# w_down's last four runs: low parts of raw blocks by DMA, and another order of the work at the ends of runs

## The chip, the cores and the metric

The kernel runs on one core of a Trainium2 chip. The metric is the device time of one execution in microseconds, here the median of several runs. A profiled execution has its own time and its own trace.

## The reference

One encoder layer on 512 tokens of width 2048, in float32: RMSNorm, one projection `w_in`, two groups of mixing heads (windowed attention at three dilations, gated linear attention in both directions), `w_out` and a residual; then RMSNorm, a SwiGLU feed-forward part and a residual; then a final RMSNorm. What matters here is the second half of the feed-forward part:

```python
h = rmsnorm(x, ffn_norm_w[l])
x = x + (jax.nn.silu(h @ w_gate[l]) * (h @ w_up[l])) @ w_down[l]
...
return rmsnorm(x, final_norm_w)
```

The hidden width is 5632, so `w_down` is 5632 by 2048 and the product to be formed is 512 x 5632 x 2048.

## The kernel before, in words

Every float32 operand of a matmul is written as a high part (a rounded copy, type float32r, made on ScalarE) and a low part (what is left, made on VectorE or by a DMA), and a product is three matmuls: high by high, high by low, low by high (lines 1591, 1592, 1593).

`w_down` is done in three stretches. Four ordinary jobs take the first four k-tiles of 128 rows, the class `Down` takes k-tiles 4 to 35 in pairs, and the last k-tiles are ordinary jobs and the tail again (`later_first`, `tail_first`). `Down` uses a scheme of Strassen's kind: a pair of k-tiles (2 x 128 rows), 512 columns of `w_down` and the 512 tokens are cut in halves each, and instead of eight block products seven are formed, of sums of blocks. Seven PSUM banks hold the seven products of one column block of 512. One **piece** is one pair of k-tiles in one column block: 7 products x 2 token halves x 3 matmuls = 42 matmuls of 128 x 256.

The pieces stand in **runs**; a run adds pieces of one column block into the seven banks. There are ten runs with 6, 6, 6, 11, 5, 5, 10, 5, 5 and 5 pieces, 64 in all (`self.runs`, `self.seq`). A column block has two runs or, in the case of blocks 1 and 2, three: the earlier ones end in `evac`, which copies each bank to SBUF and sends it to the DRAM tile `md` (added there by an accumulating DMA from the second time on); its last one, runs 6 to 9 (`summed`), begins with the sums so far, fetched from `md` (`fetch`, SyncE's queue) and copied into the banks (`preload`, ScalarE), and ends in `combine`: VectorE and ScalarE form the four output blocks from the seven banks, and `residuals` adds them to `x1`. `combine` and the `preload` of the next run alternate in the last piece of a run, since there are eight banks: a bank is refilled when `combine` has read it.

The weights of a piece go through these steps, each in buffers of the pool `s4` (20 buffers of 128 x 1024 floats):

- `load`: a raw block, 512 KB, by SyncE's queue; at most `self.most` raw blocks are alive.
- `sums(i)`: three additions on VectorE (lines 1130 to 1132) make four sums of the raw block's quarters.
- `split(i)`: high and low part of the raw block and of the sums. In the base class (lines 1142, 1147) both high parts are ScalarE copies and both low parts VectorE subtractions. For pieces for which `by_dma(i)` holds, `part(i)` has made the raw block's two parts earlier: ScalarE writes the negated rounded block (line 1481), an accumulating DMA of POOL's queue adds the raw block to it (line 1482), ScalarE writes the high part (line 1483); `split` then makes only the parts of the sums (lines 1493, 1494).
- `products(i)`: the 42 matmuls; then the piece's four part buffers go back to the pool. The raw block and the sums go back in `split`.

The pool hands out buffers in the order of the program (`Slots.get`): the first free one that was last used for the same kind, else the one free longest. An instruction that writes a buffer waits on the chip until the readers of the former content have ended, DMAs among them. Each engine and each queue works in the order in which `Down.run` issues.

`Down.run` goes over the pieces. For piece i it prepares the sums of i+2, the split of i+1 and the part of i+3, with one more of each where the pool has room, then advances `operands` (`make`; the activation's operands, which end in run 6), fetches the sums and `x1` for a run's end, issues `products(i)` and one step of `urgent` work (two `residuals`). In the last run it also begins the later jobs' weights through the stream `st`: `st.load` reads a raw block of two halves, `st.split` makes a half's parts (lines 201 and 202).

Of the kernel before, what the change touches and what calls it, by code (L numbers as in the profile page):

```python
# [114 lines left out]
def put(*slots):  # L115
    for s in slots:
        if s.home is not None:
            s.home.free.append(s.i)


def layer(nc, tc, x, attn_norm_w, w_in, rel_table, gw_f, gb_f, gw_b, gb_b, gla_norm_w, w_out,
# [4 lines left out]
    pe, act, dve, pool, sp = nc.tensor, nc.scalar, nc.vector, nc.gpsimd, nc.sync  # L126
    mm = pe.matmul

    with tc.manual_schedule(), \
# [7 lines left out]
        s4 = Slots(p4, N4, 1024, "b")  # L137
# [71 lines left out]
        st = Stream()  # L209
# [25 lines left out]
        def run_urgent():  # L235
            while urgent:
                try:
                    next(urgent[0])
                    break
                except StopIteration:  # L240
                    urgent.popleft()
# [20 lines left out]
        def job(kind, pieces, kts, acts, evac, rate=0.0, before=None, start=None, limit=None):  # L262

            j = Job()
            j.kind, j.kts, j.acts, j.evac, j.rate, j.before, j.start, j.limit = \
                kind, kts, acts, evac, rate, before, start, limit
            j.first = len(st.halves)
            st.add(pieces)
            j.n = len(st.halves) - j.first
            jobs.append(j)  # L270
            return j
# [1112 lines left out]
        def g_load(j):  # L1384
            if j < FF // 256 and j not in graw and 2 * j not in gT and j >= state["g"]:
                state["g"] = j + 1
                graw[j] = s4.get(F32, [P, 2, 512])
                sp.dma_start(out=graw[j].t.rearrange("p f t -> p (f t)"), in_=gd[j])
# [62 lines left out]
        class Down(Blocks):  # L1451
# [17 lines left out]
                return r >= 6  # L1469

            def by_dma(self, i):
                return i < self.n and self.seq[i][0] in (3, 6)

            def part(self, i):
                if not self.by_dma(i) or i in self.parts or i in self.sets:
# [92 lines left out]
            def products(self, i):  # L1568
                r, q = self.seq[i]
                c, part = self.runs[r]  # L1570
                (rh, rl), (sh, sl) = st_ = self.sets.pop(i)
                R = lambda n: (rh.t[:, 0, n], rl.t[:, 0, n])
                Z = lambda n: (sh.t[:, 0, n], sl.t[:, 0, n])
                first, last = q == part[0], q == part[-1]
                ahead = last and r + 1 < len(self.runs) and self.summed(r + 1)
                if first:
                    self.banks, self.pre = self.pre, []
                loaded = self.summed(r)
                if ahead:
                    self.preload(0)  # L1580
                x_ = self.x[q]
                prods = [(R(0), "B11"), (R(2), "B21"), (Z(2), "T2"), (Z(1), "T1"), (Z(0), "T3"), (Z(3), "B22"),
                         (R(1), "T4")]
                for n, ((wh, wl), x) in enumerate(prods):
                    if first and not loaded:
                        self.banks.append(ps.get())
                    xh, xl = x_[x]
                    for h in range(2):
                        o = self.banks[n].t[:, h * 256:(h + 1) * 256]
                        t = slice(h * P, (h + 1) * P)  # L1590
                        mm(o, xh[:, t], wh, start=first and not loaded and h == 0, stop=False, skip_group_check=True)  # L1591
                        mm(o, xh[:, t], wl, start=False, stop=False, skip_group_check=True)  # L1592
                        mm(o, xl[:, t], wh, start=False, stop=last, skip_group_check=True)  # L1593
                    if last:
                        if loaded:
                            self.combine(c, n, self.banks[n])
                        else:
                            self.evac(c, n, self.banks[n])
                        if ahead and n < 6:
                            self.preload(n + 1)  # L1600
                for hi, lo in st_:
                    put(hi, lo)
                if self.drop[q] == r:
                    put(*self.x.pop(q)["slots"])

            def evac(self, c, n, bank):

                y = s2.get()
                act.copy(y.t, bank.t)
                put(bank)  # L1610
                if (c, n) in self.seen:
                    pool.dma_start(out=md[7 * c + n], in_=y.t, accum_op=OP.add)
                else:
                    pool.dma_start(out=md[7 * c + n], in_=y.t)
                self.seen.add((c, n))
                put(y)
# [41 lines left out]
            def run(self):  # L1658
                for i, (r, q) in enumerate(self.seq):
                    c, part = self.runs[r]  # L1660
                    n = part.index(q)
                    self.load()
                    self.sums(i)
                    self.split(i)
                    self.sums(i + 1)
                    self.sums(i + 2)
                    self.split(i + 1)
                    self.part(i + 3)
                    if r not in (3, 6) and len(s4.free) > (6 if self.summed(r) else 4):
                        self.sums(i + 3)  # L1670
                        self.split(i + 2)
                    self.reserve = 11 if r in (4, 5) else 4
                    while q not in self.x:
                        self.reserve = 0
                        self.make(1)
                    self.make((r in (3, 6)) + i % 2)
                    if n == len(part) - 4 and r + 1 < len(self.runs) and self.summed(r + 1):
                        self.fetch(r + 1)
                    if self.summed(r) and n == len(part) - 2:
                        x1[c] = [s2.get() for _ in range(4)]  # L1680
                        for t in range(4):
                            pool.dma_start(out=x1[c][t].t, in_=xd[4 * c + t])
                    self.products(i)
                    run_urgent()
                    if r == len(self.runs) - 1:
                        if n == 0:
                            g_load(LAST // 2 - 2)
                        if n == 2:
                            g_split(LAST // 2 - 2)
                            g_load(LAST // 2 - 1)  # L1690
                            st.until, st.limit = None, 1
                            st.load()
                        if n > 2:
                            st.split(later_first + n - 2)
                st.limit, st.big = 3, tail_first

        def evac_later(c):
# [26 lines left out]
        later_first = len(st.halves)  # L1724
# [113 lines left out]
```

## Time and profile before

| | us |
|---|---|
| median of 3 runs | 2203.69 (2202.8 to 2204.0) |
| profiled execution | 2204.33 |
| its span, first to last instruction | 2202.6 |
| TensorE (PE) busy in the span | 2183.5 |
| VectorE (DVE) busy | 1552.0 |
| ScalarE (ACT) busy | 1201.6 |
| GpSimd (POOL) busy | 322.5 |
| `Down`, first to last matmul | 1774.9 to 2104.7 |

The granted TensorE clock was 0.998 over the span. In the rows of the table by stretches stand the stretch, its length, busy time and number of instructions (x) of PE, PEld (weight loads), DVE, ACT and POOL, then the granted clock, the DMA engines' mean busy share and GB/s. In timelines stand start, duration, engine, line, operation, output<-inputs, shapes, and in brackets the idle time before it and what ended it. In waits stand: who waited at which line <- for whom, total us, number of waits, the longest. Buffers are named by letters: `a` is the pool `s2`, `b` the pool `s4`, `pu` the PSUM banks. Matmuls are pipelined: a matmul shown with 0.28 us begins 0.12 us after the one before it.

### The profile page before, as it was taken

The page shows a single profiled execution, that of the slowest core. Times are in us where ns is not written, and L with a number is a line of the kernel's source. Part 1 is how long each engine was busy: PE and PEld are TensorE (multiplying, and loading weights), DVE is VectorE, ACT ScalarE, POOL GpSimd, SP SyncE. Part 2 cuts the span into 40 slices and gives each one's busy share as a digit, 9 for nine tenths or more (in the row PEclk, how much of TensorE's full clock was granted, in tenths as well). Part 3 has the DMA queues.
Part 4 walks back from the last instruction along what each step waited for, and adds up shares of the span by engine and source line. Part 5 has one row for each costly group of instructions (what it writes and reads, how often), then busy time and mean ns, then how long its engine had stood idle before and what let it go on. Part 6 is the DMA issues. An engine that isn't in the chain of part 4 may idle for free.

```text
span 2202.6 us, 33125 instructions
## 1 busy us (share of the span) xinstructions
PE 2183.5 (99%) x12374; PEld 1908.7 (87%) x12374; DVE 1552.0 (70%) x2699; ACT 1201.6 (55%) x2005; POOL 322.5 (15%) x356
## 2 busy tenths in 40 slices
PE   9999999999999999999999999999999999999998
PEld 7888888888888888888888888888888899999986
DVE  4366665755445446888888888888888896869975
ACT  5344444544445336666666666666666665666542
POOL 0000000000000011222222222222222112121100
PEclk9999999999999999999999999999999999999999
DMA  6525635242324434789889898898888976888642
GB/s 208 160 65 159 170 90 141 84 126 66 96 67 152 154 106 105 186 193 210 204 194 209 193 214 195 200 213 196 211 195 206 274 187 186 240 217 246 225 171 77
DMA packets 255457, 373.99 MB, mean 170 GB/s; under 512 B 17951, under 2 KB 179407, under 8 KB 255296
## 3 DMA queue, kind: packets, MB, share of 16 engines
q1 hardware_dynamic: 188768, 252.03, 36.4%
q0 software_dynamic: 65344, 118.80, 27.6%
q8 instruction: 97, 1.59, 0.3%
q10 hardware_dynamic: 1184, 1.06, 0.1%
q14 instruction: 64, 0.52, 0.1%
HBM read 246.58 MB, written 35.19 MB: 128 GB/s over the span
## 4 chain that ended last, share of the span: by engine, by line
PE 94%; DVE 3%; ACT 1%; issue 1%; DMA 1%; POOL 0%; SPq 0%; ACTq 0%; POOLq 0%; DVEq 0%
PE pd L1275 22%; PE pd L1281 11%; PE ps L303 5%; PE ps L295 5%; PE ps L305 5%; PE ps L304 5%; PE ps L296 5%; PE ps L297 5%; PE pu L1592 4%; PE pu L1591 4%; PE pu L1593 4%; PE pe L1275 4%; PE pe L1281 2%; PE ps L529 1%; PE pu L304 1%; PE pu L305 1%
## 5 line engine op out<-in xcount | busy, mean ns | idle before, releaser
L1275 PE MATMUL pd<-a,b 128*128 128x512 f32 x2112 | 528.4, 392 | 0.1
L1275 PEld LDWEIGHTS pd<-a,b 128*128 128x128 f32 x2112 | 379.0, 188 | 66.3 <-DVE a L1036 0.5
L1281 PEld LDWEIGHTS pd<-a,b 128*128 128x128 f32 x2112 | 288.5, 190 | 21.5
L1281 PE MATMUL pd<-a,b 128*128 128x256 f32 x2112 | 294.9, 282 | 0.0
L1182 POOL DMA_DIRECT2D b<-b x176 | 209.7, 1248 | 521.8 <-ACT b L1181 393.7
L202 DVE TENSOR_TENSOR a<-b,a 128x512 fp32r<-128x512 f32 x288 | 192.5, 686 | 131.1 <-ACT a L201 130.9
L1220 ACT CAST b<-b 128x1024 fp32r<-128x1024 f32 x176 | 185.4, 1053 | 166.6 <-DVE b L1206 138.4
L1592 PE MATMUL pu<-b,a 128*128 128x256 f32 x896 | 253.9, 283 | 2.4 <-DVE b L1147 1.9
L1591 PE MATMUL pu<-b,a 128*128 128x256 f32 x896 | 254.5, 284 | 1.8 <-ACT pu L1564 1.8
L1593 PE MATMUL pu<-b,a 128*128 128x256 f32 x896 | 253.5, 283 | 0.0
L1221 DVE TENSOR_TENSOR b<-b,b 128x1024 fp32r<-128x1024 f32 x176 | 214.8, 1221 | 50.7 <-ACT b L1220 26.4
L201 ACT CAST a<-b 128x512 fp32r<-128x512 f32 x288 | 169.4, 617 | 48.8 <-PE ps L305 22.3
L1591 PEld LDWEIGHTS pu<-b,a 128*128 128x128 f32 x896 | 171.9, 192 | 3.5 <-ACT pu L1564 3.5
L1592 PEld LDWEIGHTS pu<-b,a 128*128 128x128 f32 x896 | 171.9, 192 | 3.1 <-DVE b L1147 2.1
L1593 PEld LDWEIGHTS pu<-b,a 128*128 128x128 f32 x896 | 171.9, 192 | 0.0
L1303 DVE TENSOR_TENSOR a<-pd,a 128x512 f32<-128x512 f32 x132 | 91.4, 692 | 96.5 <-ACT a L1302 96.5
L1181 ACT ACTIVATE b<-b 128x768 fp32r<-128x768 f32 x176 | 149.1, 847 | 4.7 <-PE ps L305 2.9
L1183 ACT CAST b<-b 128x768 fp32r<-128x768 f32 x176 | 145.2, 825 | 0.6 <-PE ps L305 0.6
L1302 ACT COPY a<-pd 128x512 f32<-128x512 f32 x132 | 77.5, 587 | 103.2 <-PE pd L1281 103.2
L1203 DVE TENSOR_TENSOR b<-b 128x512 f32<-128x512 f32 x176 | 120.3, 684 | 0.0
L1142 ACT CAST b<-b 128x768 fp32r<-128x768 f32 x86 | 77.1, 942 | 77.6 <-issue 46.9
L593 ACT CAST b<-ps 128x512 fp32r<-128x512 f32 x64 | 37.6, 587 | 144.7 <-PE ps L529 142.8
(256 smaller groups left out, 4454.6 us busy)
## 6 DMA issues: line engine op xcount, KB each, us to landing
b<-b POOLq DMA_DIRECT2D x197, 384.0 KB, 5.4
b<-in_w_gate_dram SPq DMA_DIRECT2D x88, 512.0 KB, 3.9
b<-in_w_up_dram SPq DMA_DIRECT2D x88, 512.0 KB, 4.6
b<-in_w_down_dram SPq DMA_DIRECT2D x88, 512.0 KB, 5.6
b<-in_w_in_dram SPq DMA_DIRECT2D x48, 512.0 KB, 3.9
b<-in_w_in_dram SPq DMA_DIRECT2D x94, 256.0 KB, 4.3
b<-in_w_out_dram SPq DMA_DIRECT2D x32, 512.0 KB, 4.8
a<-a SPq DMA_DIRECT2D x96, 128.0 KB, 2.4
```

The source lines that it names most:

```text
L201: act.copy(h[2].t, r)
L202: dve.tensor_tensor(h[3].t, r, h[2].f, op=OP.subtract)
L1181: act.activation(lo.t, r, AF.Copy, scale=-1.0)
L1182: pool.dma_start(out=lo.f, in_=r, accum_op=OP.add)
L1183: act.copy(hi.t, r)
L1220: act.copy(hi.t, self.S[i].t)
L1221: dve.tensor_tensor(lo.t, self.S[i].t, hi.f, op=OP.subtract)
L1275: mm(o, wh.t[:, p, k], x_.t.rearrange("p s t -> p (s t)"), start=first and p == 0, stop=False, skip_group_check=True)
L1281: mm(o[:, 256:512], wl.t[:, p, k], x_.t[:, 0], start=False, stop=last and p == 1, skip_group_check=True)
L1591: mm(o, xh[:, t], wh, start=first and not loaded and h == 0, stop=False, skip_group_check=True)
L1592: mm(o, xh[:, t], wl, start=False, stop=False, skip_group_check=True)
L1593: mm(o, xl[:, t], wh, start=False, stop=last, skip_group_check=True)
```

## The change

Six things are changed, all in `Down` and the end of `Down.run`.

1. `by_dma` holds for all pieces of runs 6 to 9, not for those of runs 3 and 6 alone.
2. At most three raw blocks are alive in runs 6 to 9 (`self.most`), four elsewhere as before.
3. The preparation has another order there. `left` counts the pieces of the run that follow. With three, two or one left, the part of piece i+4 is made as well; with one left, the split of i+2 (the next run's first piece) as well. With none left nothing is prepared. In the first piece of runs 7, 8 and 9 one step of urgent work (two residuals) stands between the sums of i+1 and its split, and the sums of i+2 follow the split. The former extra step (sums of i+3, split of i+2) is left to runs without `left`.
4. In `evac` at the end of run 5 (`turn`) the copies of the odd products go from ScalarE to VectorE.
5. In run 9 the stream for the later jobs may hold two raw blocks instead of one.
6. There, three halves are split behind the fourth piece's products, instead of one behind the fourth and one behind the fifth.

```diff
             def by_dma(self, i):
-                return i < self.n and self.seq[i][0] in (3, 6)
+                return i < self.n and (self.seq[i][0] == 3 or self.summed(self.seq[i][0]))
...
-                            self.evac(c, n, self.banks[n])
+                            self.evac(c, n, self.banks[n], ahead)
...
-            def evac(self, c, n, bank):
+            def evac(self, c, n, bank, turn):
 
                 y = s2.get()
-                act.copy(y.t, bank.t)
+                if turn and n % 2:
+                    dve.tensor_copy(y.t, bank.t)
+                else:
+                    act.copy(y.t, bank.t)
                 put(bank)
...
                     n = part.index(q)
+                    left = len(part) - 1 - n if self.summed(r) else None
+                    self.most = 3 if left is not None else 4
                     self.load()
                     self.sums(i)
                     self.split(i)
-                    self.sums(i + 1)
-                    self.sums(i + 2)
-                    self.split(i + 1)
-                    self.part(i + 3)
-                    if r not in (3, 6) and len(s4.free) > (6 if self.summed(r) else 4):
-                        self.sums(i + 3)
-                        self.split(i + 2)
+                    if left == 0:
+                        pass
+                    elif r > 6 and n == 0:
+                        self.sums(i + 1)
+                        run_urgent()
+                        self.split(i + 1)
+                        self.sums(i + 2)
+                        self.part(i + 3)
+                    else:
+                        self.sums(i + 1)
+                        self.sums(i + 2)
+                        self.split(i + 1)
+                        self.part(i + 3)
+                        if left in (1, 2, 3):
+                            self.part(i + 4)
+                        if left == 1:
+                            self.split(i + 2)
+                        elif left is None and r != 3 and len(s4.free) > 4:
+                            self.sums(i + 3)
+                            self.split(i + 2)
...
-                            st.until, st.limit = None, 1
+                            st.until, st.limit = None, 2
                             st.load()
-                        if n > 2:
-                            st.split(later_first + n - 2)
+                        if n == 3:
+                            st.split(later_first + 3)
```

## The prediction

> **What bounds the kernel now.** I read the page first: its head and the busy times.
>
> ```profile
> span 2202.6 us, 33125 instructions
> PE 2183.5 (99%) x12374; PEld 1908.7 (87%) x12374; DVE 1552.0 (70%) x2699; ACT 1201.6 (55%) x2005; POOL 322.5 (15%) x356
> ```
>
> TensorE is the bound, so a change to other engines can only remove, or add, moments in which TensorE waits. Next the table by stretches, cut at the ends of runs. I number w_down's 64 pieces 0 to 63; run 6 is pieces 39 to 48, run 7 is 49 to 53, run 8 is 54 to 58, run 9 is 59 to 63. The first row is an undisturbed stretch, the others are runs 6, 7, 8 and 9.
>
> ```profile
> 1805.12:1905.92 100.80, 100.80 (x843) 100.80 (x841) 77.18 (x122) 59.40 (x85) 19.41 (x30) 1.00 0.76 219
> 1971.44:2023.78 52.34, 51.52 (x422) 50.62 (x421) 41.51 (x72) 37.33 (x57) 15.49 (x21) 1.00 1.03 288
> 2023.78:2051.14 27.36, 25.46 (x213) 25.26 (x211) 26.62 (x39) 14.12 (x19) 1.61 (x3) 1.00 0.53 181
> 2051.14:2077.95 26.81, 26.03 (x212) 25.40 (x211) 24.90 (x37) 14.12 (x19) 1.61 (x3) 1.00 0.62 198
> 2077.95:2104.72 26.77, 26.06 (x213) 25.43 (x212) 20.97 (x31) 13.08 (x19) 3.19 (x6) 1.00 0.74 246
> ```
>
> 100.80 us hold 20 pieces (840 matmuls, and three of a neighbour), so a piece of 42 matmuls takes 5.04 us and a matmul 0.12. Run 6 should take 50.40 us and the others 25.20 each: they lose 1.94, 2.16, 1.61 and 1.57 us, 7.28 together. The waits between 1971 and 2113 say on what, and the timeline of TensorE shows one more loss right behind run 9:
>
> ```profile
> PEld pu L1591 <- ACT pu L1564: 3.5, 8, 0.8
> PEld pu L1592 <- DVE b L1147: 2.1, 1, 2.1
> ```
>
> ```profile
> 2104.70 0.40 PE L303 MATMUL pu<-a,a 128*128 128x512 f32 x1
> ...
> 2107.45 0.39 PE L303 MATMUL pu<-a,a 128*128 128x512 f32 x1
> 2108.75 0.50 PE L304 MATMUL pu<-a,a 128*128 128x512 f32 x1 [0.92 <-DVE a L202]
> ...
> 2111.89 0.50 PE L304 MATMUL pu<-a,a 128*128 128x512 f32 x1
> ```
>
> Twelve matmuls take 2.75 us (2104.70 to 2107.45), 0.229 each; the 25 up to 2111.89 should take 5.73 and take 7.19: 1.5 us lost. So 8.8 us in all are there to be won, 0.4% of the span; a difference of 0.2% (4.4 us) is about what a measurement can tell from none.
>
> VectorE's timeline shows how the loss arises (starts, durations; the combination runs from the first L1621 to the last L1622, L1652 are the residuals, L1130 opens the sums of a piece, L1147 and L1494 are low parts):
>
> ```profile
> 1977.92 1.23 DVE L1494 TENSOR_TENSOR b<-b,b 128x1024 fp32r<-128x1024 f32 x1 [7.37 <-ACT b L1493]
> ...
> 2021.18 0.68 DVE L1621 TENSOR_TENSOR b<-pu,a 128x512 f32<-128x512 f32 x1
> ...
> 2027.14 1.42 DVE L1652 SCALAR_TENSOR_TENSOR a<-b,small,a 128x512 f32<-128x512 f32 x2
> 2028.47 0.69 DVE L1130 TENSOR_TENSOR b<-b 128x512 f32<-128x512 f32 x1
> ...
> 2030.00 2.09 DVE L1147 TENSOR_TENSOR b<-b,b 128x768 fp32r<-128x768 f32 x2
> ...
> 2051.44 0.68 DVE L1621 TENSOR_TENSOR b<-pu,a 128x512 f32<-128x512 f32 x1
> ...
> 2078.19 0.68 DVE L1621 TENSOR_TENSOR b<-pu,a 128x512 f32<-128x512 f32 x1
> ...
> 2101.37 0.69 DVE L1621 TENSOR_TENSOR b<-pu,a 128x512 f32<-128x512 f32 x1 [3.48 <-PE pu L1593]
> ```
>
> In run 9, where nothing is in the way, the first add stands 3.33 us before the run's end (2101.37 against 2104.70). In runs 7 and 8 it comes 0.30 and 0.24 us after the end, so 3.63 and 3.57 us late, and the next run loses 1.61 and 1.57. In run 6 it is 0.73 late (2021.18 against 2023.78 less 3.33) and its successor's first piece loses nothing; there the 2.1 us are the second piece's wait for its low part. So **lateness of the combination is free up to 2.0 us, and costs one for one beyond**.
>
> **The change, part by part.** *Copies of run 5's end.* ScalarE's copies into and out of PSUM there form one chain:
>
> ```profile
> 1969.02 0.58 ACT L1564 COPY pu<-a 128x512 f32<-128x512 f32 x1
> 1969.54 0.58 ACT L1609 COPY a<-pu 128x512 f32<-128x512 f32 x1
> ...
> 1976.84 1.05 ACT L1493 CAST b<-b 128x1024 fp32r<-128x1024 f32 x1
> 1977.79 0.85 ACT L1481 ACTIVATE b<-b 128x768 fp32r<-128x768 f32 x1
> ...
> 1991.19 0.85 ACT L1481 ACTIVATE b<-b 128x768 fp32r<-128x768 f32 x1 [2.66 <-DMA b<-in_w_down_dram]
> ...
> 1992.67 1.13 ACT L1537 CAST a<-a 128x512 fp32r<-128x512 f32 x2
> ...
> 2100.58 0.59 ACT L1627 COPY a<-pu 128x512 f32<-128x512 f32 x1 [5.59 <-PE pu L1593]
> ```
>
> Fourteen copies take 7.82 us, 0.56 each. Three move to VectorE (nearest row: L1621 reading PSUM, 0.68 each, 2.0 us), which idles 7.37 us there; that cover is large. ScalarE is free 1.6 us earlier, at 1975.2. TensorE's waits for L1564 in piece 39 and for the low part behind L1493 in pieces 40 and 41 go: together 1.4 of run 6's 1.94 us. The last 0.5 is another wait, in the chain of waits:
>
> ```profile
> 1978.93 9.56 DMA b<-b
> 1988.54 0.38 PE pu L1592
> ```
>
> The DMA that makes piece 42's low part lands 9.56 us after its issue. It moves 1.6 us forward, TensorE 1.4: about 0.3 us of this wait stay.
>
> *Behind run 9.* Three halves are split before the last piece instead of one before and one behind it, with two loads in flight. VectorE's three L202 go under the fourth piece. The 1.5 us go; if ScalarE were 2 us late there, they would stay.
>
> *Low parts by DMA in runs 7 to 9.* VectorE loses one of the two L1147 per piece (2.09 the pair), 15 times, and ScalarE gets two operations (1.48 from 1991.19 to 1992.67) for one, POOL a DMA issue, the DMA engines 384 KB. On engines' busy time this fits: VectorE was busy 26.62 of 27.36 and 24.90 of 26.81 us in runs 7 and 8, ScalarE at 14 of 27 us, DMA at 0.53 and 0.62. What remains is order and waiting.
>
> *VectorE's order at a run's end.* With T the run's end, the combination starts at T-3.33 if ScalarE is in time, and takes 5.96 us (2021.18 to 2027.14): T+2.63. Then come, in the new order, two residuals (1.33, from 2027.14 to 2028.47), the sums of the new run's second piece (1.53, to 2030.00), two residuals (1.33), its low part (1.22): T+8.04. TensorE wants it at its third product's second matmul, 13 matmuls into the second piece: T+5.04+1.56 = T+6.60. So **1.44 us are lost at each of the three run ends** even if nothing is late; the two pieces ready ahead are the last piece and the new run's first, not its second. With lateness L of ScalarE, the first piece loses L-2.0 beyond 2.0 and the second 1.44 and the smaller of L and 2.0: **a run end costs 1.44+L**.
>
> *Three raw blocks instead of four, and parts a step earlier.* Here I expect the loss. `most` falls to 3. I followed the pool's free list by hand: the buffer that this frees at piece 39 is taken by an operand's load, so raw block j always reuses the buffer of block j-3. That is free only when block j-3's low-part DMA, which reads it, has landed. SyncE's waits between 1955 and 2080 show that this is a real wait already with four; then the latencies in runs 6 (1988 to 2009) and 3 (1860 to 1920), medians from issue to landing at the end of each row:
>
> ```profile
> SPq L1114 <- DMA b<-b: 28.3, 8, 8.4
> ```
>
> ```profile
> b<-in_w_down_dram SPq DMA_DIRECT2D x5, 512.0 KB, 5.7
> b<-b POOLq DMA_DIRECT2D x4, 384.0 KB, 7.3
> ```
>
> ```profile
> b<-in_w_down_dram SPq DMA_DIRECT2D x11, 512.0 KB, 5.1
> b<-b POOLq DMA_DIRECT2D x9, 384.0 KB, 7.5
> ```
>
> A loop from one part to the next in the same buffer: L1481 0.85, 0.29 to POOL's issue (1977.79+0.85 to 1978.93), 7.3 or 7.5 to landing, 5.7 or 5.1 for the new block: 14.1 in run 6, 13.7 in runs like run 3, which has this traffic. Three pieces are 15.12 us. That is enough for a steady step, but in the last four pieces of a run `part(i + 4)` wants the part a step (5.04 us) earlier, and ScalarE, in order, then stands before an unlanded block (as at 1991.19 already). Queued behind it: the high part of the new run's first piece, the preloads and the first copy of the combination (L1627), for which VectorE waits.
>
> Run 6: ScalarE starts part 42 at 1975.2+0.95 = 1976.2; part 45 at 1976.2+0.85+0.29+9.56+5.7 = 1992.6; part 48 at 2006.8; part 51, wanted in piece 47, at 2020.9. Then 1.48 for it, 0.95 for the high part, 0.52 for a preload: L1627 at 2023.9. The run ends at 1971.44+50.40+0.3 = 2022.1, and L1627 should stand 4.12 before (2100.58 against 2104.70): 2018.0. L = 5.9; cost 7.3.
> Run 7: the sums of piece 50 end at T+2.63+5.9+1.33+1.53 = T+11.4; block 53 lands at T+16.5, its part starts, part 56 at T+30.2, L1627 at T+33.2. The run ends at T+25.2+7.3 = T+32.5, L1627 due at T+28.4: L = 4.8, cost 6.2. Run 8, in the same way: sums at 10.3, 15.4, 29.1, 32.1 against 31.4-4.12: L = 4.8, cost 6.2.
>
> **Sum**: new losses 0.3+7.3+6.2+6.2 = 20.0 against 8.8: +11.2 us on the profiled execution's 2204.33 (1.7 around the span). That lies 0.64 above the median 2203.69 of the runs, so on the median 2214.9.
>
> **Bounds.** The loop is the unknown. Over the whole kernel the two DMAs took (least, median, longest; L1482 first, L1114 next):
>
> ```profile
> DMA to landing us min/median/max: 3.8/7.4/9.6
> ```
>
> ```profile
> DMA to landing us min/median/max: 3.3/4.5/12.7
> ```
>
> With 3.8 and 3.3 no part is late. The other end is the busiest stretch, run 6 up to where run 7's first loads begin (again L1482 first):
>
> ```profile
> DMA to landing us min/median/max: 6.1/7.6/9.6
> ```
>
> ```profile
> DMA to landing us min/median/max: 4.3/6.8/12.7
> ```
>
> With 7.6 and 6.8 the loop is 15.5 us: run 6's end becomes about 4 us dearer and the later two about 3.5 each, +22. I take the medians of run 6 and run 3, since these stages have the same transfers.
> [...]
>
> **Rivals.** 1. *Short latencies*: lower DMA load than in run 6 (0.53 against 1.03) speaks for it; then only VectorE's order costs: 0.3+3*1.44 = 4.6 against 8.8, 2199.5. Against: five more 384 KB transfers per run. 2. *Half late*: TensorE's own stalls give the loop time, L near 1.5 each: 4.6+4.5, 2204. 3. *Faster, the other side*: VectorE's relief is the whole story; its place is the run ends, its price 8.5, and it decides if the second piece's low part comes by T+6.60, 1.44 us earlier than I sum: 2195.2. For it: VectorE's busy share in run 7. Against: the row of 5.96 us and the order of the residuals. 4. *Worse*: DMA full, loops of 15.5: 2225.
>
> **Numbers.** Forecast 0.52 (own range 2209 to 2220), rivals 0.18, 0.14, 0.07, 0.09. Rival 1 lies at the edge of 0.2%: a third of it counts as faster. Faster 0.07+0.05 = 0.12, same 0.13+0.14 = 0.27, slower 0.52+0.09 = 0.61. Range 2199 to 2222, leaving out rival 3 and most of 4.
>
> **What will show it.** Right: idle time of ScalarE before L1481 put down to DMA of w_down or L1114 on SyncE waiting for b<-b in runs 7 and 8; L1627 after T-4.12; TensorE waiting at a run's second piece for L1494. Wrong: ScalarE never waiting for w_down, or no loss at the second pieces (5.04 us each).

## The result, and the profile after

The changed kernel takes 2226.59 us (median of 4 runs, 2225.61 to 2228.66) against 2203.85 of the kernel before beside it: 1.0103 times the time, 95% interval 1.0091 to 1.0115. That is 22.7 us slower. The profiled execution took 2225.61 us, 21.3 more than that of before. The head of its page and its busy times:

```profile
span 2223.8 us, 33168 instructions
PE 2190.6 (99%) x12374; PEld 1915.4 (86%) x12374; DVE 1542.0 (69%) x2687; ACT 1210.6 (54%) x2017; POOL 335.8 (15%) x371
```

VectorE has 10.0 us less to do and ScalarE 9.0 more, as the change says. TensorE is busy 7.1 us longer with the same 12374 matmuls; this is its clock, as shown below. The other 14 of the 21 us are on balance waits, of which busy times tell nothing. The table by stretches does; its rows are runs 6, 7, 8 and 9 (all engines):

```profile
1971.00:2031.59 60.59, 54.11 (x423) 53.10 (x422) 42.71 (x75) 40.18 (x61) 15.92 (x20) 0.94 0.95 236
2031.59:2065.60 34.01, 28.81 (x213) 27.92 (x211) 19.80 (x31) 17.14 (x24) 6.49 (x9) 0.90 0.82 232
2065.60:2100.43 34.83, 28.46 (x212) 27.51 (x211) 20.34 (x31) 17.31 (x24) 6.50 (x9) 0.90 0.77 209
2100.43:2127.53 27.10, 25.72 (x212) 25.32 (x211) 21.88 (x34) 13.75 (x20) 6.09 (x10) 1.00 0.78 258
```

At 5.04 us a piece the runs should take 50.40 and three times 25.20; they lose 10.2, 8.8, 9.6 and 1.9 us, 30.5 together, where they lost 7.3 before. The same view for TensorE alone (stretch, length, busy time, granted clock, DMA share, GB/s) shows in which pieces: the first row is piece 42, the next three are the last pieces of runs 6, 7 and 8, the fifth row is a part of piece 48 and the last the first piece of run 8.

```profile
1986.12:1993.07 6.95, 5.30 (x45) 1.00 1.00 224
2018.97:2031.59 12.62, 7.96 (x45) 0.73 0.71 185
2052.74:2065.60 12.86, 8.14 (x45) 0.73 0.93 266
2087.65:2100.43 12.78, 7.71 (x44) 0.73 0.89 249
2026.50:2031.50 5.00, 5.00 (x27) 0.54 0.99 281
2066.00:2070.00 4.00, 4.00 (x35) 1.00 0.01 4
```

The three last pieces lose 7.6, 7.8 and 7.7 us, piece 42 loses 1.9, and what remains of the 30.5 is spread in smaller amounts, the largest 1.9 and 1.35 in pieces 60 and 55. TensorE waits twice in a last piece, inside it and not at its end; its timeline in piece 48:

```profile
2020.29 0.28 PE L1593 MATMUL pu<-b,a 128*128 128x256 f32 x1
2023.10 0.39 PE L1591 MATMUL pu<-b,a 128*128 128x256 f32 x1 [2.53 <-ACT b L1493]
2025.62 0.58 PE L1592 MATMUL pu<-b,a 128*128 128x256 f32 x1 [2.13 <-DVE b L1494]
```

By starts, the third product's first matmul is 2.69 us late and the next 2.40 more. The remaining loss of piece 48, 2.49 us, is the clock: the row that begins at 2026.50 holds 27 matmuls in 5.00 us at a granted clock of 0.54, where 0.12 each would give 41. ScalarE, which the first of these waits names, shows what it had waited for; then the groups of waits from 1971 to 2130 and, in the last row, those of SyncE from 1955 to 2110:

```profile
2019.50 0.85 ACT L1481 ACTIVATE b<-b 128x768 fp32r<-128x768 f32 x1 [6.59 <-DMA b<-in_w_down_dram]
2020.25 0.81 ACT L1483 CAST b<-b 128x768 fp32r<-128x768 f32 x1
2020.97 1.13 ACT L1537 CAST a<-a 128x512 fp32r<-128x512 f32 x2
2022.01 1.04 ACT L1493 CAST b<-b 128x1024 fp32r<-128x1024 f32 x1
```

```profile
ACT b L1481 <- DMA b<-in_w_down_dram: 36.7, 9, 8.3
PE pu L1591 <- ACT b L1493: 11.2, 4, 4.4
PE pu L1592 <- DVE b L1494: 6.3, 7, 2.1
```

```profile
SPq L1114 <- DMA b<-b: 68.1, 15, 12.6
```

The group of 36.7 us was 2.7 us before. At 2019.50 ScalarE begins the part of piece 50, the second of the three parts (pieces 49, 50 and 51) that are wanted a step early; it had stood 6.59 us for that piece's raw block, and behind it in its order stands the high part of piece 48's own sums (L1493 at 2022.01). So the last piece of the run waits for a block of the second piece after it. Why the block is late stands in SyncE's timeline and, for the two loads named last, in the chain of waits:

```profile
2004.27 4.25 SPq L1560 DMA_DIRECT2D a<-md  x7
2009.56 30.92 SPq L1114 DMA_DIRECT2D b<-in_w_down_dram  x5
2040.58 5.28 SPq L1560 DMA_DIRECT2D a<-md  x7
2046.04 8.69 SPq L1114 DMA_DIRECT2D b<-in_w_down_dram  x3
```

```profile
2009.56 9.83 DMA b<-in_w_down_dram
2046.04 9.56 DMA b<-in_w_down_dram
```

Right ahead of this load stand the seven fetches of the next run's sums (L1560). A load issued behind them takes 9.8 and 9.6 us to land, against the 5.7 and 5.1 of the medians that the prediction used. That a load waits there for the 7 x 256 KB ahead of it is, so far, a reading of the order in this timeline; what the place of the fetches is worth was measured by moving them (below: 8.4 us, with four raw blocks 16.9). The fetches do not do it alone: in the kernel before, the loads issued 1.5 and 1.3 us behind the last fetch for runs 8 and 9, with no low parts by DMA around them, landed after 5.7 and 6.6 us. The one behind the fetches for run 7, where low parts are made by DMA already in the kernel before, took 12.7; that is the longest time in the prediction's own rows.

At the start of run 8 the DMA engines are almost idle (0.01 from 2066 to 2070), while they are at 0.71 to 0.93 in the last pieces, where TensorE waits. This speaks against a volume that is too large and for transfers that are asked for in bunches; the experiments test it.

### The profile page after: what moved, and what is told of

The parts are those of the page before. It is cut to its first block, busy times and chain, and to the rows that moved or that the text cites. A ratio compares the mean times of both kernels' runs of the same rounds, so it can differ in the third digit from the quotient of the medians.

```text
span 2223.8 us, 33168 instructions
## 1 busy us (share of the span) xinstructions
PE 2190.6 (99%) x12374; PEld 1915.4 (86%) x12374; DVE 1542.0 (69%) x2687; ACT 1210.6 (54%) x2017; POOL 335.8 (15%) x371
## 4 chain that ended last, share of the span: by engine, by line
PE 91%; DMA 3%; DVE 3%; ACT 2%; issue 1%; POOL 0%; ACTq 0%; SPq 0%; DVEq 0%; POOLq 0%
PE pd L1275 22%; PE pd L1281 11%; PE ps L303 5%; PE ps L305 5%; PE ps L304 5%; PE ps L295 5%; PE ps L297 5%; PE ps L296 5%; PE pe L1275 4%; PE pu L1592 3%; PE pu L1593 3%; PE pu L1591 3%; PE pe L1281 2%; DMA b<-in_w_down_dram 2%; PE ps L529 1%; PE pu L304 1%
## 5 line engine op out<-in xcount | busy, mean ns | idle before, releaser
L1591 PE MATMUL pu<-b,a 128*128 128x256 f32 x896 | 257.3, 287 | 11.2 <-ACT b L1493 11.2
L1592 PE MATMUL pu<-b,a 128*128 128x256 f32 x896 | 258.3, 288 | 8.2 <-DVE b L1494 6.3
L1593 PE MATMUL pu<-b,a 128*128 128x256 f32 x896 | 256.7, 287 | 0.0
L1591 PEld LDWEIGHTS pu<-b,a 128*128 128x128 f32 x896 | 175.3, 196 | 12.1 <-ACT b L1493 12.0
L1592 PEld LDWEIGHTS pu<-b,a 128*128 128x128 f32 x896 | 175.3, 196 | 10.6 <-DVE b L1494 8.7
L1593 PEld LDWEIGHTS pu<-b,a 128*128 128x128 f32 x896 | 175.4, 196 | 0.0
L1183 ACT CAST b<-b 128x768 fp32r<-128x768 f32 x176 | 145.4, 826 | 0.6 <-PE ps L305 0.6
L295 PE MATMUL ps<-a,a 128*128 128x512 f32 x288 | 115.5, 401 | 0.0
```

Source lines behind the costliest of these rows:

```text
L295: mm(o, wh.t[:, c], xh.t, start=first, stop=False)
```

## The experiments

Three causes stood to be told apart: the supply of raw blocks (three alive instead of four, parts a step early, the place of the fetches in SyncE's queue), VectorE's order at a run's end, and TensorE's clock after a stall. Losses below are, as above, each piece's time from its first matmul to the next piece's first, less 5.04 us, added up by place; each ratio is against runs of before beside the kernel (medians 2203.64 to 2204.22):

| kernel | median us | ratio, 95% interval | 39-44 | 45-50 | 51-55 | 56-63 |
|---|---|---|---|---|---|---|
| before | 2203.85 | | 1.9 | 2.1 | 1.6 | 1.6 |
| after | 2226.59 | 1.0103 (1.0091 to 1.0115) | 2.2 | 8.3 | 9.8 | 10.2 |
| e1_raw4 | 2224.92 | 1.0092 (1.0078 to 1.0106) | 4.5 | 8.1 | 9.1 | 7.3 |
| e2_part4_last | 2223.95 | 1.0088 (1.0073 to 1.0103) | 2.2 | 7.3 | 11.1 | 8.8 |
| e3_dma_parts_alone | 2211.92 | 1.0035 (1.0021 to 1.0049) | 2.1 | 2.3 | 4.6 | 5.4 |
| e4_copies_and_tail | 2204.11 | 1.0001 (0.9993 to 1.0010) | 4.2 | 3.6 | 0.3 | 1.6 |
| e6_fetch_first | 2218.18 | 1.0060 (1.0044 to 1.0077) | 5.2 | 9.1 | 3.5 | 7.5 |
| e7_raw4_fetch_first | 2208.03 | 1.0015 (1.0006 to 1.0025) | 6.8 | 1.6 | 1.9 | 3.9 |
| e8_four_of_five | 2202.76 | 0.9994 (0.9985 to 1.0003) | 5.2 | 1.5 | 0.4 | 0.5 |
| e9_order_alone | 2207.56 | 1.0013 (1.0004 to 1.0022) | 2.1 | 4.3 | 4.3 | 2.8 |
| e10_five_fetch_first | 2202.93 | 0.9996 (0.9987 to 1.0005) | 1.5 | 1.6 | 1.6 | 1.6 |
| e11_four_fetch_first | 2201.06 | 0.9982 (0.9974 to 0.9991) | 2.7 | 0.4 | 0.4 | 0.5 |
| e12_no_dma_fetch_first | 2202.57 | 0.9994 (0.9985 to 1.0003) | 2.4 | 3.6 | 0.3 | 1.5 |

### Four raw blocks up to two pieces before a run's end

```diff
-                    self.most = 3 if left is not None else 4
+                    self.most = 3 if left in (0, 1) else 4
```

> The changed kernel with one thing undone: four raw blocks may be alive in runs 6 to 9 again, except in the last two pieces of a run, where the pool has no room. Theory S (too few raw blocks: ScalarE stands before L1481 until a block has landed, because its buffer is still read by the low-part DMA of the block three before): ScalarE's wait for w_down falls from 36.7 us to under 10, the last pieces of runs 6, 7 and 8 lose under 2 us each instead of 7.6, 7.8 and 7.7, the clock stays whole, and the time is 2202 to 2208. Rival D (the low-part DMAs of runs 7 to 9 are too much for the DMA engines, however many blocks there are): still above 2220. Rival O (the order of the work at the ends of runs costs it): still above 2220, since the order is the same.

It gains under 2 us. ScalarE's wait falls by half, but the loss goes from inside the last pieces to the second pieces behind the run ends, 50, 55 and 60, which lose 6.3, 6.2 and 3.6. The group of waits, TensorE's timeline in piece 50 and a load behind the fetches in the chain of waits:

```profile
ACT b L1481 <- DMA b<-in_w_down_dram: 19.3, 5, 8.0
```

```profile
2035.36 0.38 PE L1591 MATMUL pu<-b,a 128*128 128x256 f32 x1 [2.08 <-ACT b L1493]
2036.74 0.58 PE L1592 MATMUL pu<-b,a 128*128 128x256 f32 x1 [1.00 <-DVE b L1494]
```

```profile
2044.34 11.31 DMA b<-in_w_down_dram
```

The load behind the fetches still takes 11.3 us. At the ends of runs 7 and 8 ScalarE stands 7.1 and 8.0 us before a part whose block has not landed; at the end of run 6 it no longer waits for a block, but 6.1 us for a matmul, so for the part's buffer. Either way ScalarE reaches the combination late (its first copy begins 0.1 to 0.5 us ahead of the next run's first matmul, and is due 4.12 ahead), and VectorE passes that on. By starts the two stalls are 2.24 and 1.26 us, 3.5 together; the rest of the 6.3 and 6.2 is the clock. So three raw blocks alone are not the cause.

### The part a step earlier only once

```diff
-                        if left in (1, 2, 3):
+                        if left == 1:
                             self.part(i + 4)
```

> The changed kernel with three raw blocks, but the part of piece i+4 is made early only where one piece of the run is left, not where two or three are. Theory S: the block that ScalarE waits for now stands behind the high part of the run's last piece, not ahead of it, so the 5 us waits inside the last pieces go; the combination comes late instead (3 to 6 us), as the prediction's sum had it: 2208 to 2218. If the early parts are the whole cause, so that three blocks cost nothing without them: 2200 to 2205. Rival D: no change, 2224 to 2229.

It gains 2.6 us, far less than expected. The last pieces of runs 6, 7 and 8 lose only 1.5, 3.0 and 0.7 us now, and the combinations are late in their place (first copy 0.1 us ahead of the next run's first matmul in all three); piece 50 waits at the same matmuls and as long as in the experiment before:

```profile
2036.49 0.38 PE L1591 MATMUL pu<-b,a 128*128 128x256 f32 x1 [2.08 <-ACT b L1493]
2037.88 0.38 PE L1592 MATMUL pu<-b,a 128*128 128x256 f32 x1 [1.00 <-DVE b L1494]
```

ScalarE's wait for w_down is still 32.4 us. The part a step early only decides in which piece ScalarE's lateness is paid; it does not make it.

### Low parts by DMA alone, in the kernel before

```diff
-                return i < self.n and self.seq[i][0] in (3, 6)
+                return i < self.n and (self.seq[i][0] == 3 or self.summed(self.seq[i][0]))
```

> The kernel before with one part of the change alone: low parts of raw blocks by DMA in runs 7 to 9 too, in the old order and with four raw blocks. Theory S: no wait of ScalarE for w_down over 3 us in runs 7 to 9, and a time within 5 us of before, 2199 to 2208. Rival D: 2215 or more, with ScalarE or TensorE waiting for the DMAs in runs 7 to 9.

With the order, four raw blocks and all else of before, this edit alone costs 8.3 us. ScalarE's timeline at the end of run 7:

```profile
2049.20 0.85 ACT L1481 ACTIVATE b<-b 128x768 fp32r<-128x768 f32 x1 [2.90 <-DMA b<-in_w_down_dram]
2049.95 0.82 ACT L1483 CAST b<-b 128x768 fp32r<-128x768 f32 x1
2050.67 0.58 ACT L1564 COPY pu<-a 128x512 f32<-128x512 f32 x1
2051.19 0.58 ACT L1627 COPY a<-pu 128x512 f32<-128x512 f32 x1
```

The wait for the block stands ahead of the preload and of the combination's first copy (L1627 here as in the kernel before). VectorE's first add waits for that copy (idle 4.25 us before 2051.80), and behind the combination now stands the low part of the second piece, which the kernel before made ahead of it: pieces 55 and 60 lose 2.27 and 3.76 us (1.6 of the latter by the clock), where they lost nothing before. This is the predicted mechanism; it needs neither three blocks nor the new order. The time lies between the two ranges expected.

### The copies of run 5's end and the tail alone, in the kernel before

```diff
-                act.copy(y.t, bank.t)
+                if turn and n % 2:
+                    dve.tensor_copy(y.t, bank.t)
+                else:
+                    act.copy(y.t, bank.t)
...
-                            st.until, st.limit = None, 1
+                            st.until, st.limit = None, 2
                             st.load()
-                        if n > 2:
-                            st.split(later_first + n - 2)
+                        if n == 3:
+                            st.split(later_first + 3)
```

> The kernel before with two parts of the change alone: the odd copies at the end of run 5 on VectorE, and the later jobs' halves split behind the fourth piece of run 9 with two blocks in flight. By the prediction's terms run 6 loses 0.3 to 0.5 us instead of 1.94, and the 1.5 us behind run 9 go: 3 us less than before, 2200.5 to 2201.5. No theory of the slowdown has these two parts in it; were one of them harmful, the time would be above 2204.

No change in all, where 3 us less were expected. The tail gives its 1.6 us (from the end of `Down` to the last instruction 96.2 us instead of 97.9), but the copies give nothing. Pieces 39 to 41 lose 0 instead of 1.4 us; piece 42 loses 4.2, a wait of 2.66 and 1.6 by the clock. The chain of waits of the changed kernel, then that of this experiment, and this experiment's run 6 by stretches, which begins at 1969.75:

```profile
1976.63 11.38 DMA b<-b
```

```profile
1975.38 12.23 DMA b<-b
```

```profile
1969.75:2024.39 54.64, 52.13 (x422) 51.93 (x421) 43.47 (x76) 35.65 (x54) 15.50 (x21) 0.97 1.00 276
```

Before, this DMA landed 17.05 us after run 6's start (1978.93 + 9.56 less 1971.44), in the changed kernel 17.01 (1976.63 + 11.38 less 1971.00), here 17.86. Counted from run 6's start it is issued 1.9 us earlier in both (5.63 us behind it instead of 7.49), and it lands when it landed before or later; from its issue to its landing the DMA share is 1.10 in the kernel before and 1.11 in the changed kernel, over the whole of run 6 here 1.00 (the row above), and POOL issues the DMAs of run 5's seven products ahead of it (from 1970.41 before, from 1969.97 in the changed kernel). What TensorE wins in pieces 39 to 41 it waits at piece 42.

### The clock by itself

In the kernel before, the subtraction that makes the low part of the sums is done five, seven and nine times over in pieces 3, 9 and 15, so that TensorE has to wait there.

```diff
-                    dve.tensor_tensor(lo.t, src, hi.f, op=OP.subtract)
+                    for _ in range({3: 5, 9: 7, 15: 9}.get(i, 1) if len(out_) else 1):
+                        dve.tensor_tensor(lo.t, src, hi.f, op=OP.subtract)
```

> The kernel before, with waits put where it has none: in pieces 3, 9 and 15 VectorE makes the low part of the sums 5, 7 and 9 times over (1.22 us each, the same values), which is 4.9, 7.3 and 9.8 us more; the output is unchanged. The disputed cost by itself: what TensorE's clock adds to a wait of some length. Theory C (a wait of several us halves the granted clock for one or two stretches of 3.4 us, as the records of the changed kernel show it): the longest gap is followed by matmuls at 0.21 us instead of 0.12 and 1.5 to 3 us of loss beside the gap, the shortest by none; the sum of the losses is larger than the gaps by 2 to 5 us. Without such an effect the losses are the gaps alone, and the slow matmuls in the changed kernel come from somewhere else.

The median is 2211.79 us, 1.0033 times before (1.0021 to 1.0045). The waits that this puts in did not come out in the order of the repetitions, since VectorE was not equally far ahead in the three pieces: none, 3.44 us and 1.78 us. Behind the 1.78 the clock stays; behind the 3.44 it falls. TensorE by stretches, around piece 9: the stall, 3.40 us behind it, and the time after that.

```profile
1819.80:1823.30 3.50, 0.22 (x3) 0.99 0.00 0
1823.40:1826.80 3.40, 3.40 (x17) 0.52 0.00 0
1826.90:1833.00 6.10, 6.10 (x54) 1.00 0.50 142
```

17 matmuls in 3.40 us instead of 28: a stall of 3.44 us cost 5.02 in all.

### The fetches ahead of the loads

The fetches of the next run's sums go from a run's fourth piece from its end, where they are issued behind that piece's preparation, to the top of the fifth piece from its end, ahead of its load. First in the changed kernel, then with the four raw blocks of the first experiment as well.

```diff
                     n = part.index(q)
+                    if n == len(part) - 5 and r + 1 < len(self.runs) and self.summed(r + 1):
+                        self.fetch(r + 1)
...
-                    if n == len(part) - 4 and r + 1 < len(self.runs) and self.summed(r + 1):
-                        self.fetch(r + 1)
```

> The changed kernel with the seven fetches of the next run's sums moved from a run's fourth piece from the end, where they stand ahead of the weight loads of the last pieces on SyncE's queue, to the top of its fifth from the end (the first piece of runs 7 and 8), where the DMA engines were 0.01 to 0.26 busy. Theory F (the blocks that ScalarE waits for land late, 9.6 to 10.7 us after issue, since seven times 256 KB go in front of them): those loads land in 4 to 7 us, ScalarE's wait for w_down falls from 36.7 to under 20, the last pieces of runs 7 and 8 lose 0 to 3 us instead of 7.8, and the time is 2206 to 2216. Theory S (three blocks, whatever the fetches do): 2222 or more.

> The changed kernel with both: four raw blocks except in a run's last two pieces, and the fetches moved to the fifth piece from the end. Theory F and S together: no wait of ScalarE for w_down over 2 us in runs 7 and 8, the combination in time, and of the run ends only VectorE's order is left, 1.5 to 3.5 us each: 2203 to 2210. If the low-part DMAs themselves set the pace (rival D): 2215 or more.

The place of seven transfers in SyncE's queue is worth 8.4 us (2226.59 to 2218.18), with four blocks 16.9 (2224.92 to 2208.03). By itself it does less than expected: 2218.18 lies above its range, and ScalarE still waits 22.7 us for w_down. With both, ScalarE's wait for w_down is 4.0 us instead of 36.7, and behind run 6's first pieces only pieces 50, 55 and 60 lose anything: 1.57, 1.88 and 3.93. The group of waits and piece 50 in TensorE's timeline:

```profile
ACT b L1481 <- DMA b<-in_w_down_dram: 4.0, 3, 2.4
```

```profile
2036.02 0.39 PE L1592 MATMUL pu<-b,a 128*128 128x256 f32 x1 [0.99 <-DVE b L1494]
```

With the supply in time, what is left is VectorE's order, at the predicted matmul of the second piece and close to the predicted 1.44 us; piece 60's 3.93 are a stall of 2.34 and the clock. The same transfers are made as in the changed kernel, so their volume is not the cause. The fetches of run 6 were moved too, and piece 42, which waits for its DMA, now loses 6.8; the old order shows the same below (e8 against e11).

### The order without the low parts by DMA

The changed kernel, with `by_dma` as before:

```diff
-                return i < self.n and (self.seq[i][0] == 3 or self.summed(self.seq[i][0]))
+                return i < self.n and self.seq[i][0] in (3, 6)
```

> The changed kernel with its first part alone undone: low parts by DMA only in runs 3 and 6, as before; order, three blocks, copies and tail as changed. The order's own price: VectorE comes to the second piece's low parts at T+6.82 and has two to make (2.09), the first wanted at T+5.16, so each of the three run ends costs about 2.6 us, run 6's beginning about 4, and 1.6 are won behind run 9: 2205 to 2210, and no wait of ScalarE for w_down over 3 us in runs 7 to 9. If the order is what costs the 22 us, 2218 or more.

As expected: slower by 3.3 us, with the second pieces 2.66 us late, since VectorE has both low parts of each piece to make. TensorE's first wait of piece 50, then pieces 50, 55 and 60 by stretches:

```profile
2030.94 0.54 PE L1592 MATMUL pu<-b,a 128*128 128x256 f32 x1 [2.50 <-DVE b L1147]
```

```profile
2028.16:2037.46 9.30, 6.80 (x44) 0.82 0.23 74
2057.62:2066.92 9.30, 6.80 (x44) 0.82 0.25 60
2087.08:2094.90 7.82, 5.30 (x45) 1.00 0.72 250
```

The order alone, with the copies and the tail, costs 3.3 us and the DMA parts alone 8.3. The two together cost 11 us more than the sum (22.7 less 11.6): the order asks for the parts earlier, and the fetches and the third block's limit make the blocks come later.

### Low parts by DMA in the old order, with the fetches first

From the kernel before, all with the changed tail. e8: low parts by DMA in runs 7 to 9 except each run's third piece, the fetches of runs 6 to 9 moved. e11: the same, the fetches of run 6 in their old place. e10: as e11, but with the DMA parts of all five pieces. e12: as e11, without any DMA part in runs 7 to 9. The core of e11:

```diff
-                return i < self.n and self.seq[i][0] in (3, 6)
+                return i < self.n and (self.seq[i][0] in (3, 6) or self.summed(self.seq[i][0]) and self.runs[self.seq[i][0]][1].index(self.seq[i][1]) != 2)
...
+                    if n == len(part) - 5 and r in (6, 7, 8):
+                        self.fetch(r + 1)
...
-                    if n == len(part) - 4 and r + 1 < len(self.runs) and self.summed(r + 1):
+                    if n == len(part) - 4 and r == 5:
                         self.fetch(r + 1)
```

> The kernel before, in its old order and with four raw blocks, with low parts by DMA in runs 7 to 9 for all pieces but the third of a run (the one whose part would stand in a run's last piece, ahead of the combination on ScalarE), the fetches moved as above, and the tail's part of the change. If parts that ScalarE has to make at a run's end are what makes the combination late: the run ends lose under 2.5 us each, 2199 to 2204. If DMA parts are dear in themselves: 2208 or more.

> The kernel before, old order, four raw blocks, low parts by DMA for all five pieces of runs 7 to 9 (as in the run that made these parts alone, 2211.9), with the fetches of runs 7, 8 and 9 moved to the fifth piece from the run's end and the tail's part. Theory F: the part in a run's last piece no longer waits for its block, L1627 comes 1 to 2 us late by ScalarE's own work, the run ends cost 1.5 to 3 us each: 2202 to 2206. If the fetches' place does not matter in this order: 2209 to 2211 (1.6 less than without the tail's part).

> The kernel before with the same moved fetches and the tail's part, and low parts by DMA for the pieces of runs 7 to 9 but the third of each run; the fetch of run 6 stays in its old place, unlike in the earlier run of this kind, where run 6's beginning lost 5.16 us. Run 6 should lose 2 again, the three run ends 2.4 together as there, and the time be 2199 to 2201, the lowest so far.

> The same without low parts by DMA in runs 7 to 9: the kernel before with the moved fetches and the tail's part alone. If the low parts by DMA are what shortens the run ends there (VectorE 0.95 us less per piece), the run ends lose 5.3 us as before and the time is 2202 to 2203; if the moved fetches do it, it is as fast as with them, 2199 to 2201.

The moved fetches turn the DMA parts from a loss of 8.3 us into nothing (e3 against e10; in the profiled executions 8.1 of it lie in `Down` and 1.0 behind it, with the tail). e11 is the version that beats both kernels: 2201.06 us, 0.9982 of before (0.9974 to 0.9991), 1.1% below the changed kernel. Its run 6 and its runs 7 to 9 by stretches:

```profile
1972.47:2025.59 53.12, 51.54 (x422) 1.00 1.04 273
2025.59:2051.33 25.74, 25.58 (x213) 1.00 0.97 276
2051.33:2076.91 25.58, 25.56 (x212) 1.00 0.96 289
2076.91:2102.50 25.59, 25.57 (x212) 1.00 0.81 251
```

Runs 7 to 9 lose 0.5, 0.4 and 0.4 us, where they lost 2.2, 1.6 and 1.6 in the kernel before. The DMA parts themselves are worth little in all: without any (e12) the median is 1.5 us higher, and the two intervals overlap. The traces show two sides of it. In `Down` e11 loses 4.0 us and e12 7.9. Behind it, e11 takes 97.7 us to the last instruction and e12 96.2: in e11 TensorE waits there for VectorE (0.91 us before 2109.49), and most of what the tail's change gave is lost.

e10 loses 1.6 us at each second piece, waiting for VectorE's low part, and e11 only 0.3 to 0.4. The two differ in the third piece's part alone. In e10 its two operations stand on ScalarE ahead of the combination's first copy in the run's last piece, and VectorE's first add waits for that copy: at run 7's end it begins 1.96 us ahead of the end, in e11 3.33. The fetch of run 6 is better left where it was (e8: 5.2 us lost in pieces 39 to 44, e11: 2.7).

## Why the prediction was right or wrong

The direction was right, and so was the cause: raw blocks land too late, and ScalarE, in order, stands before them. The path on which TensorE pays for it was another, and the size was twice the forecast (+22.7 against +11.2), above the range. The time lies near that of rival 4 (2225), but not by its way, since the DMA engines are not full throughout.

- **"It moves 1.6 us forward, TensorE 1.4: about 0.3 us of this wait stay"** failed. The copies made ScalarE earlier as said, and pieces 39 to 41 lose nothing. But the DMA for piece 42 was not limited by its issue: it landed at the same time, so the gain came back there. In pieces 39 to 44 2.2 us were lost instead of 0.3. The error was to carry a latency of 9.56 us along with the issue, in a stretch whose DMA share is 1.1: issued 1.9 us earlier, it took 11.38.
- **Behind run 9, "the 1.5 us go"**: right. From the end of `Down` to the last instruction it is 96.31 us instead of 97.86, 1.55 less.
- **Busy time fits**: right, and it decided nothing: VectorE is busy 19.80 of run 7's 34.01 us, and the DMA share goes from 0.93 to 0.01 within two pieces.
- **ScalarE stands before L1481 in front of an unlanded block, behind SyncE's wait for b<-b**: right. ScalarE's group grew from 2.7 to 36.7 us, SyncE's from 28.3 to 68.1 (1955 to 2080 before, 1955 to 2110 after).
- **"I followed" the chain of blocks 42, 45, 48 and 51 with medians of 5.7 and 5.1 us**: this step failed. The chain itself came near in run 6 (part 51 begins at 2022.95, in the sum at 2020.9), but it was not the one that decides. That is the block of piece 50, 55 and 60, whose load stands behind the seven fetches and lands after 9.6 us and more; the fetches did not stand in the sum. L1493 of the run's last piece stands behind that part, so TensorE waits inside the last piece, 5.1 to 5.7 us by starts. The sum had only the combination as the way of the loss, and that was not late: its first add begins 4.6, 3.6 and 3.0 us ahead of the three run ends (due 3.33, free up to 2.0 later), and the first pieces of runs 7 to 9 lose nothing. Without the clock the run ends lost 5.8, 7.2 and 8.1 us instead of 7.3, 6.2 and 6.2 (8.3, 9.8 and 10.2 less 2.49, 2.60 and 2.05): that the sum is near is luck. Moving the fetches and leaving four blocks took 18.6 of the 22.7 us away, which shows the cause; taking away only the third block's limit or only the early parts did not.
- **VectorE's order, "1.44 us are lost at each of the three run ends"**: right in place and size, 1.57 and 1.88 where the supply was in time. **"a run end costs 1.44+L"**: right where the combination is late at all. In e1 its first copy is 3.7, 4.7 and 5.5 us late (counted from where the run would end without the wait for the preload), the new run's first piece, with the wait right ahead of it, loses 1.8, 2.8 and 3.7 (the sum: 2.0 less than L), and the stalls of the second pieces are 3.5 each time (the sum: 3.44).
- **Not in the sum**: the clock. Three stretches at half clock cost 7.1 us in the changed kernel. This is most of what the forecast lacked: the losses come to 30.5 us, 23.4 without the clock, against the forecast's 20.0.
- Of the signs named in the prediction, the waits of ScalarE and SyncE showed. The combination's first copy (L1627, here L1630) begins 5.6, 4.6 and 4.0 us ahead of the run ends, due at 4.12, so this sign did not. The wait at the second pieces showed only in small (1.35 and 1.90 in pieces 55 and 60), since VectorE had its time while TensorE stood inside the last pieces.

## What to carry to other kernels

Price a DMA by what stands ahead of it in its queue and by how full the engines are at that time, not by a median; here the loads behind seven fetches took 9.6 us and more in the changed kernel against medians of 5.7 and 5.1, and a DMA that was issued 1.9 us earlier, at a DMA share of 1.1, landed no earlier. Where a wait of one engine is moved, list everything that stands behind it in that engine's timeline (here L1493, behind 6.59 us) up to the next instruction on which the bounding engine hangs, for every block that is late and not only for one chain. And before adding transfers, look whether a few others, wanted later, can be moved out of the way: here seven fetches, one piece earlier, took away the whole 8.3 us that the low parts by DMA had cost.

## What was not expected of the hardware

A stall of a few us cost TensorE more than its length in several places, as with the 5.02 us for one of 3.44 above. Behind some stalls in these traces the granted clock falls to half for 3.41 or 6.83 us, with a matmul each 0.21 us instead of 0.12, and about 1.6 us are lost on top behind 3.41, 2.0 to 2.8 behind 6.83. The gap of 1.78 us in the run that puts waits in did not do it; the pairs of 5.1 to 5.7 us in the last pieces did. Between them it varies: of three gaps of 2.66 us in the rows of the order without DMA parts, two halved the clock (9.30 us for the piece, 0.82) and one did not (7.82 us, 1.00); in the kernel before, a gap of 2.05 us ahead of piece 50 did not, in three experiments one of 2.05 or 2.06 did.

The clock's own record in the traces shows what goes with it. In the changed kernel it falls to half at 2024.29, 2058.42 and 2092.55 us and stays there for 6.83 us each time; in the kernel before it is at half from 8.57 to 11.98 and from 2196.51 on. Within each of the two traces these steps lie whole multiples of 3.413 us apart (2, 10, 12, 20 and 22 of them from the first in the changed kernel, 1 and 641 in the kernel before). They do not stand at one distance from the gaps: the three falls come 3.72, 4.08 and 3.30 us behind the end of the last matmul ahead of the first gap in a last piece. Below, a window is one such stretch of 3.413 us between two places where the clock could step by this count. The first two rows are two such windows of the kernel before, the one that holds most of the gap ahead of piece 50's wait and the next; the other two are the same of the experiment with the copies.

```profile
2029.26:2032.67 3.41, 1.67 (x14) 1.00 0.28 102
2032.67:2036.08 3.41, 3.41 (x31) 1.00 0.30 112
2029.71:2033.13 3.42, 1.52 (x13) 1.00 0.24 67
2033.13:2036.54 3.41, 3.41 (x18) 0.50 0.38 139
```

The same gap leaves TensorE idle for 1.74 us of the window in the one and for 1.90 in the other, since in the kernel before the gap begins in the window ahead. In the 14 traces together, from 15 to 2185 us, 22 windows at full clock have 1.89 us or more of idle time, and half clock follows each; 8849 have 1.77 or less, and it follows none. Of these the changed kernel's trace has three of the former, with 3.03, 3.25 and 3.30 us of idle time, and together with that of the kernel before 1261 of the latter, with 1.74 or less. The clock stays halved for a second window where the stall reaches into the first (0.62 us or more of idle time there, ten windows of ten; 1.33, 0.80 and 1.77 in the changed kernel). So in these traces a gap of 2 to 3.5 us cost 1.6 us more or nothing by where it fell in the windows, which begin at 2029.26 us from the span's start in the one trace above and at 2029.71 in the other, and a difference of that size between two traces here can come from it alone. A later wait can give it back: piece 54 loses 1.6 us in the kernel before and 0.3 in the three experiments whose clock fell at piece 50.
